# Seven half-size products in place of eight for the gate and up blocks of a two-layer diffusion backbone

## The chip, the cores and the metric

The kernel runs on one core of one Trainium2 chip. The time is the device time of one execution in microseconds (us), from runs of the whole program; the profile is one execution recorded by the hardware profiler. Engines are named as in the profile: PE (TensorE), PEld (its weight loads), DVE (VectorE), ACT (ScalarE), POOL (GpSimd) and SP (SyncE, which issues the DMAs).

## The reference

Two layers of a backbone over 640 tokens: 512 latent tokens and 128 context tokens, 1024 features each, which share all weights. Cut to what the change touches:

```python
D_MODEL = 1024; FFN_HIDDEN = 2816
def layer(x, cvec, p, rope, ctx_kv):
    sh1, sc1, g1, sh2, sc2, g2 = split(silu(cvec) @ p['w_ada'] + p['b_ada'], 6)
    h = rmsnorm(x, p['norm1_g']) * (1 + sc1) + sh1
    out, k, v = mixer(h, p, rope, ctx_kv)      # pooling, convolution, attention, gates, w_o
    x = x + g1 * out
    h2 = rmsnorm(x, p['norm2_g']) * (1 + sc2) + sh2
    ffn = (silu(h2 @ p['w_gate']) * (h2 @ p['w_up'])) @ p['w_down']
    return x + g2 * ffn, k, v
```

All of it is fp32. The last layer's output goes through one more norm.

## The kernel before

**Layout.** Activations lie transposed: features on the 128 partitions in 8 chunks (`KC`), the 640 tokens along the free axis, in two parts, `HALF` (384 and 256 tokens). A matmul takes 128x128 weights and one chunk of one part.

**Three products for one.** An fp32 value v is kept as a pair of fast-type (fp32r) numbers: hi = v rounded to that type, lo = v - hi. A product of two such values is taken as hi·hi + lo·hi + hi·lo, so each 128x128 weight tile and each activation chunk cost three matmuls per token part (`mm_op`, L425). The hi part is a cast on ACT (L365 for weights, L293 and L296 for activations), the lo part a subtraction, mostly on DVE (L369, L294, L297).

**Weights** stream in as blocks of 128 output columns (`Unit`, list `plan`): a DMA of 512 KB into one of 3 `RAW` buffers, then the split into one of 3 `WHL` slots, then 48 matmuls (8 chunks, 3 products, 2 parts). Blocks are used in the order of the plan.

**Feed-forward.** `w_gate` and `w_up` have 22 blocks each. `GROUPS` cuts them into 8, 8 and 6: in a group each gate block and its up block give two PSUM tiles, `hidden` turns them into one chunk of silu(gate)·up (tanh on ACT L1627, DVE L1628, DVE L1633, split L296 and L297), and then 8 blocks of `w_down` take the group's chunks to the residual stream, where DVE adds them with the gate factor (L1264, one instruction for the 512 latent and one for the 128 context tokens).

**Around it.** Ahead of the feed-forward stands a norm (`norm_half`, `norm_chunk`) that is taken part by part: while PE works on the residual blocks' second part, the first part's norm runs on DVE, ACT and POOL. `first_units` then takes three blocks (gate 0, up 0, gate 1) chunk by chunk as the norm delivers. The adaLN vectors of what is still to come (`ada_back`, L495: a 128x512 DVE instruction that multiplies and sums, and a small read of its accumulator behind it) are made during layer 0: 320 such instructions, put where DVE has nothing else.

**What sets the order.** Every engine's instruction order is fixed when the program is built: `_Order` runs a plain model of costs, and each engine takes the most urgent of the instructions that the model finds ready. Weight splits have a slack of 1500 ns (`WEIGHT`), ada work one of 1e7 (`BACK`), so it goes last. `dve_pool` lets the model choose between DVE and POOL by which would finish first. On the chip each engine follows its fixed list and waits on semaphores.

Of the kernel before, what the change touches and what calls it, by code (L numbers as in the profile page):

```python
# [1767 lines left out]
```

## Time and profile before

| | |
|---|---|
| time, median of 3 runs | 1947.42 us (1944.76 to 1949.25) |
| profiled execution: span, first to last instruction | 1945.7 us (1.7 us under the median) |
| PE busy | 1893.2 us, 97% |
| DVE, ACT, POOL busy | 1180.7, 651.3, 214.2 us |
| matmuls at L425 | 11520 of 12893 |
| span that the feed-forward stages take | about 433 us in layer 0, 442 us in layer 1 |

The time of the profiled execution apart from its span is not listed; the three runs lie within 0.23%. Read the table stage by stage: a busy share is a mean over stages in which different engines come last. A matmul's listed duration contains its pipeline, so the pace of PE is read from the starts of successive matmuls.

### The profile page before, as it was taken

Reading aid. Unit: us, or ns where it says so; the run is one execution under the profiler, and the core shown is the slowest. Engines: PE = TensorE matmul, PEld = TensorE weight load, DVE = VectorE, ACT = ScalarE, POOL = GpSimd, SP = SyncE. Lnnn points to the kernel's source line nnn. Section 1 sums busy time; section 2 is a strip of 40 time slices with the busy share of each in tenths; the row PEclk is TensorE's granted clock in tenths of the full one; section 3 lists DMA queues with packets and bytes.
Section 4 is the critical chain, followed back from the end, with each engine's and each line's share of the span. In section 5 each row is a group of like instructions: output and inputs, shape, how many; then the busy total and the mean of one; then the engine's idle time right before and its main releaser. Section 6 shows DMA issues by size and latency. Waiting matters only on the chain.

```text
span 1945.7 us, 31187 instructions
## 1 busy us (share of the span) xinstructions
PE 1893.2 (97%) x12893; PEld 1861.3 (96%) x12893; DVE 1180.7 (61%) x1998; ACT 651.3 (33%) x1039; POOL 214.2 (11%) x182
## 2 busy tenths in 40 slices
PE   6999999999999999999989999999999999999997
PEld 4888999999999999999989899999999999999997
DVE  7689868878777777763477985333347333333334
ACT  4466732222432122212244664222224221221223
POOL 3352000001200000000035400000012000000001
PEclk8999999999999999999998999999999999999998
DMA  7210135446234444432322101222322222222212
GB/s 274 96 46 29 44 122 159 159 157 212 92 128 148 148 147 153 150 130 71 116 80 70 41 28 44 86 72 77 115 97 76 77 73 71 74 76 76 77 60 71
DMA packets 74223, 195.79 MB, mean 101 GB/s; under 512 B 8545, under 2 KB 12641, under 8 KB 74081
## 3 DMA queue, kind: packets, MB, share of 16 engines
q1 hardware_dynamic: 74082, 193.81, 30.2%
q8 instruction: 101, 1.65, 0.4%
q14 instruction: 40, 0.33, 0.1%
HBM read 186.96 MB, written 5.51 MB: 99 GB/s over the span
## 4 chain that ended last, share of the span: by engine, by line
PE 85%; DVE 10%; issue 2%; ACT 2%; POOL 0%; DMA 0%; SPq 0%; DVEq 0%; ACTq 0%; POOLq 0%
PE ps L425 79%; PE ps L957 1%; PE ps L939 1%; DVE g L294 1%; PE ps L977 1%; DVE g L683 1%; DVE z L661 1%; DVE st L945 1%; DVE g L495 1%; PE ps L1412 1%; PE ps L750 1%; DVE t L641 0%; DVE z L791 0%; ACT p L947 0%; DVE p L276 0%
## 5 line engine op out<-in xcount | busy, mean ns | idle before, releaser
L425 PE MATMUL ps<-g,wh 128*128 128x256 f32 (+1 forms) x7552 | 1680.4, 310 | 3.4 <-DVE g L294 1.7
L425 PEld LDWEIGHTS ps<-g,wh 128*128 128x128 f32 x7552 | 1279.7, 190 | 4.9 <-issue 3.1
L425 PE MATMUL ps<-g,wl 128*128 128x384 f32 (+1 forms) x3776 | 1167.3, 309 | 1.9 <-DVE wl L369 1.9
L425 PEld LDWEIGHTS ps<-g,wl 128*128 128x128 f32 x3776 | 717.3, 190 | 2.5 <-DVE wl L369 2.4
L365 ACT CAST wh<-wr 128x1024 fp32r<-128x1024 f32 (+2 forms) x256 | 250.8, 981 | 546.2 <-PE ps L425 291.8
L369 DVE TENSOR_TENSOR wl<-wr,wh 128x1024 fp32r<-128x1024 f32 (+2 forms) x233 | 275.5, 1182 | 115.9 <-ACT wh L365 108.9
L1264 DVE SCALAR_TENSOR_TENSOR g<-ps,mod,g 128x128 f32<-128x128 f32 (+2 forms) x140 | 67.3, 518 | 166.1 <-PE ps L425 166.0
L495 DVE CUSTOM_DVE_ANT_0 junk<-p,k,vec 128x512 f32<-128x512 f32 x160 | 122.5, 766 | 33.8 <-DMA p<-in_w_ada 31.7
L495 DVE CUSTOM_DVE_ANT_0 junk<-p,k,part 128x512 f32<-128x512 f32 x160 | 120.2, 751 | 22.4 <-DMA p<-in_w_ada 18.1
L588 POOL TENSOR_TENSOR u<-u,t 128x256 f32<-128x256 f32 (+1 forms) x15 | 17.8, 1189 | 941.9 <-ACT t L583 941.9
L1633 DVE TENSOR_TENSOR t<-t,ps 128x640 f32<-128x640 f32 x44 | 36.1, 821 | 133.5 <-PE ps L425 133.5
L1628 DVE SCALAR_TENSOR_TENSOR t<-t,ps 128x640 f32<-128x640 f32 x44 | 35.9, 821 | 124.9 <-ACT t L1627 124.9
L1627 ACT ACTIVATE t<-ps 128x640 f32<-128x640 f32 x44 | 30.9, 707 | 220.2 <-PE ps L425 220.2
L1214 ACT ACTIVATE t<-ps 128x640 f32<-128x640 f32 x32 | 22.6, 707 | 192.0 <-PE ps L425 192.0
L1225 POOL TENSOR_TENSOR u<-u,t 128x640 f32<-128x640 f32 x12 | 22.8, 1903 | 516.3 <-ACT wh L365 268.8
L367 POOL TENSOR_TENSOR wl<-wr,wh 128x1024 fp32r<-128x1024 f32 x23 | 57.9, 2519 | 91.8 <-ACT wh L365 67.4
L947 ACT ACTIVATE p<-ps,st 128x640 f32<-128x640 f32 x64 | 50.9, 795 | 38.8 <-DVE st L945 34.4
L294 DVE TENSOR_TENSOR g<-ps,g 128x640 fp32r<-128x640 f32 (+1 forms) x68 | 54.8, 811 | 11.9 <-ACT g L293 11.5
L659 ACT ACTIVATE g<-t,mod,gain 128x128 fp32r<-128x128 f32 (+2 forms) x88 | 46.5, 574 | 32.7 <-DVE gain L1425 17.9
L425 PE MATMUL ps<-g,g 128*128 128x384 f32 (+1 forms) x192 | 45.5, 338 | 11.7 <-DVE g L683 6.6
L945 DVE TENSOR_REDUCE st<-ps 128x1 f32<-128x640 f32 x64 | 51.8, 815 | 6.5 <-PE ps L939 6.1
L641 POOL TENSOR_TENSOR t<-g,u 128x256 f32<-128x256 f32 (+2 forms) x37 | 50.0, 1355 | 44.4 <-DVE z L661 9.2
(146 smaller groups left out, 1292.0 us busy)
## 6 DMA issues: line engine op xcount, KB each, us to landing
p<-in_w_ada SPq DMA_DIRECT2D x160, 256.0 KB, 3.0
wr<-in_w_in SPq DMA_DIRECT2D x76, 512.0 KB, 3.4
wr<-in_w_gate SPq DMA_DIRECT2D x44, 512.0 KB, 3.3
wr<-in_w_up SPq DMA_DIRECT2D x44, 512.0 KB, 3.4
wr<-in_w_down SPq DMA_DIRECT2D x32, 512.0 KB, 3.3
g<-in_w_ada SPq DMA_DIRECT2D x16, 512.0 KB, 5.8
wr<-in_w_br SPq DMA_DIRECT2D x32, 256.0 KB, 2.7
wr<-in_w_o SPq DMA_DIRECT2D x16, 512.0 KB, 3.6
```

What stands on the lines that cost most here:

```text
L294: yield dve(n, lambda: nc.vector.tensor_sub(lo, src, hi))
L365: yield act(n, lambda: nc.scalar.copy(h, r), slack=WEIGHT)
L367: yield pool(n, lambda: nc.gpsimd.tensor_sub(w, r, h), slack=WEIGHT)
L369: yield dve(n, lambda: nc.vector.tensor_sub(w, r, h), slack=WEIGHT)
L425: nc.tensor.matmul(toks(ps, c0, n), lhsT=wt[:, c], rhs=xt[:, c0 : c0 + n], start=start and i == 0, stop=stop and i == 2,)
L495: return dve(n + 60, lambda: nc.vector.tensor_tensor_reduce(out=waste[:, :n], in0=w, in1=s, scale=0.5, scalar=start, op0=ALU.mult, op1=ALU ...
L641: f = lambda e: e.tensor_mul(t[:, :n], xk, r)
L659: nc.scalar.activation(out, sl, AF.Identity, bias=bias, scale=scale)
L945: yield dve(TOK, lambda: nc.vector.tensor_reduce(st[:, 0:1], toks(ps), axis=AX.X, op=ALU.max, negate=True))
L947: yield act(TOK + 140, lambda: nc.scalar.activation(pp, toks(ps), AF.Exp, bias=st[:, 0:1], accum_out=st[:, 1:2]))
L1264: yield dve(n, lambda: nc.vector.scalar_tensor_tensor(xs, toks(ps, s0, n), mods[l][:, v, seg * KC + m : seg * KC + m + 1], xs, op0=ALU.mul ...
L1633: yield dve(TOK, lambda: nc.vector.tensor_mul(t, t, toks(ps)))
```

## The change

`HALF` becomes 320 and 320 tokens; the norm's second and first parts of 320 are covered by three 128-token tiles each (`TILES`, two of them overlapping in the first part). `GROUPS` becomes 6, 6, 6, 4. From the third gate block on, a gate block and its up block are no longer two products. Stacked, they form a 2x2 block matrix: rows gate and up, columns the first and the last 512 input features (a11, a12, a21, a22); the activations form a 2x2 block matrix of feature halves by token parts (b11 to b22). Strassen's scheme in Winograd's form takes the block product with seven products of 4 chunks by 320 tokens instead of eight.

New work for that: per layer the sums t1 to t4 of the activations (`Quarters.combine`, split in `Quarters.parts`); per pair the sums s1 to s4 of the weights (`Pair.sums`), split as seven 512-wide quarters instead of two 1024-wide blocks (L351, L355); per pair the gathering of the results (`Seven.gather`): partial sums accumulate in PSUM, and in between are copied by ACT (L642) and added by DVE (L647). PE's product 6 waits for the copy of product 1, product 4 for the addition of product 7. `hidden_of` takes silu(gate)·up from the gathered tile.

The weight slots become 6 slots of 4 KB per partition (`WQ`; a pair needs 7, an ordinary block 2), raw buffers 4 instead of 3, large tiles 13 instead of 12. Comments are removed throughout, and those lines are left out here.

```diff
-HA = 384
+HA = 320
...
-GROUPS = ((0, 8), (8, 8), (16, 6))
+GROUPS = ((0, 6), (6, 6), (12, 6), (18, 4))
+PLAIN = 2
...
+TILES = {(0, TOK): (0, P, 2 * P, 3 * P, 4 * P), HALF[0]: (0, P, HA - P), HALF[1]: (HA, 3 * P, 4 * P)}
...
-    BIG, RAW, WHL, TT, ZZ, PP, UU, PS, MIX = (_Slots(order, n) for n in (12, 3, 3, 3, 2, 2, 4, 4, 1))
+    BIG, RAW, WQ, TT, ZZ, PP, UU, PS, MIX = (_Slots(order, n) for n in (13, 4, 6, 3, 2, 2, 4, 4, 1))
...
+    class Pair:
...
+        ORDER = ("a11", "s1", "s2", "a12", "s3", "s4", "a22")
...
+        def prepare(self, turn):
+            for e in self.loaded:
+                yield e
+            (_, r0), (_, r1) = self.raw
+            h = D // 2
+            self.part = {"a11": r0[:, :h], "a12": r0[:, h:], "a21": r1[:, :h], "a22": r1[:, h:]}
+            self.there = {q: event() for q in ("s1", "s2", "s3", "s4")}
+            self.parted = {q: event() for q in self.ORDER}
+            spawn(self.sums())
+            yield turn
+            for q in self.ORDER:
+                s = self.slot[q] = yield WQ.get()
+                t = mk("wq", s, (D,), F32R)
+                self.hi[q], self.lo[q] = t[:, :h], t[:, h:]
+                spawn(self.parts(q))
+            self.placed.fire()
+            for e in self.parted.values():
+                yield e
+            for s, _ in self.raw:
+                RAW.put(s)
+        def sums(self):
+            n = D // 2
+            p = self.part
+            freed = {"s1": ("s2",), "s2": ("s4",), "s3": (), "s4": ()}
+            for q, x, y, op in (
+                ("s1", "a21", "a22", ALU.add), ("s2", "s1", "a11", ALU.subtract),
+                ("s3", "a11", "a21", ALU.subtract), ("s4", "a12", "s2", ALU.subtract),
...
+                p[q] = u_t(s)[:, :n]
+                f = lambda e: e.tensor_tensor(p[q], p[x], p[y], op=op)
+                yield dve_pool(n, f, slack=WEIGHT)
+                self.there[q].fire()
+                after([self.parted[q]] + [self.there[r] for r in freed[q]], lambda s=s: UU.put(s))
+        def parts(self, q):
+            if q in self.there:
+                yield self.there[q]
+            yield from half_split(self.hi[q], self.lo[q], self.part[q], D // 2)
+            self.parted[q].fire()
+            self.ready[q].fire()
...
+        def free(self, q):
+            WQ.put(self.slot[q])
...
+            for j in range(g0, g0 + gn):
+                if j < PLAIN:
+                    plan += [Unit(a["w_gate"][l, j], big=j == 0), Unit(a["w_up"][l, j])]
+                else:
+                    plan.append(Pair(a["w_gate"][l, j], a["w_up"][l, j]))
             plan += [
-                Unit(a[n][l, g0 + j], big=g0 + j == 0 and n == "w_gate")
-                for j in range(gn) for n in ("w_gate", "w_up")
-            ]
-            plan += [
-                Unit(a["w_down8"][l, gi, m] if gn == 8 else a["w_down6"][l, m], gn * P) for m in range(KC)
+                Unit(a["w_down6"][l, gi, m] if gn == 6 else a["w_down4"][l, m], gn * P) for m in range(KC)
...
+    class Quarters:
...
+        def make(self):
+            self.z = []
+            for _ in range(2):
+                s = yield BIG.get()
+                self.zslots.append(s)
+                self.z.append(big_t(s, F32))
...
+        def combine(self):
...
+            steps = (("t1", "b12", "b11", "b11"), ("t2", "b22", "t1", None), ("t3", "b22", "b12", "b12"),
+                     ("t4", "b21", "t2", "b21"))
...
+                for c in (slice(0, 2), slice(2, 4)):
+                    yield dve_pool(2 * HA, lambda e: e.tensor_sub(b[q][:, c], b[x][:, c], b[y][:, c]))
+                split_up.append(spawn(self.parts(q, b[q])))
+            for d in split_up:
+                yield d
+            for z in self.zslots + [s]:
+                BIG.put(z)
+            self.freed.fire()
...
+        def parts(self, q, src):
+            s = yield BIG.get()
+            self.slots.append(s)
+            t = big_t(s).rearrange("p a b -> p (a b)").rearrange("p (i k n) -> p i k n", i=2, k=4)
+            self.tiles[q] = t
+            for c in (slice(0, 2), slice(2, 4)):
+                yield act(2 * HA, lambda: nc.scalar.copy(t[:, 0, c], src[:, c]))
+                yield dve(2 * HA, lambda: nc.vector.tensor_sub(t[:, 1, c], src[:, c], t[:, 0, c]))
+            self.ev[q].fire()
...
+    def product(out, w, q, x, t, start, stop):
...
+        done = event()
+        def f(k):
+            for i, (wt, lo) in enumerate(((w.hi, 0), (w.lo, 0), (w.hi, 1))):
+                nc.tensor.matmul(
+                    out, lhsT=wt[q][:, k * P : k * P + P], rhs=x.get(t, lo, k),
+                    start=start and k == 0 and i == 0, stop=stop and k == 3 and i == 2, skip_group_check=True,
+                )
+        for k in range(4):
+            yield pe(3 * HA, lambda: f(k), slack=MAIN, follow=True, done=done if k == 3 else None)
+        after([done], lambda: w.free(q))
+        return done
...
+        def run(self, x):
+            w = next(coming)
+            self.s0 = yield PS.get(0)
+            s1 = yield PS.get(0)
+            p0, p1 = ps_t(self.s0), ps_t(s1)
+            pa, pb, pc = p0[:, :HA], p0[:, 512 : 512 + HA], p1[:, :HA]
+            self.pa = pa
+            got = {n: event() for n in range(1, 8)}
...
+            def go(n, out, q, t, start, stop, wait=None):
+                if wait:
+                    yield kept[wait]
+                d = yield from product(out, w, q, x, t, start, stop)
+                after([d], got[n].fire)
+            yield from go(1, pa, "a11", "b11", True, True)
+            yield from go(5, pc, "s1", "t1", True, True)
+            yield from go(6, pa, "s2", "t2", False, True, 1)
+            yield from go(2, pb, "a12", "b21", True, True)
+            yield from go(7, pa, "s3", "t3", False, True, 6)
+            yield from go(3, pc, "s4", "b22", False, True, 5)
+            yield from go(4, pa, "a22", "t4", False, True, 7)
+            after([got[4]], self.c21.fire)
...
+        def gather(self, got, kept, pa, pb, pc, s1):
...
+            def keep(n, dst, src):
+                yield got[n]
+                yield act(HA, lambda: nc.scalar.copy(dst, src))
+                kept[n].fire()
+            def plus(n, dst, src):
+                yield got[n]
+                yield dve(HA, lambda: nc.vector.tensor_add(dst, dst, src))
+            def c11():
+                yield from keep(1, lo, pa)
+                yield from plus(2, lo, pb)
+            def c22():
+                yield from keep(5, y, pc)
+                yield from plus(7, y, pa)
+                kept[7].fire()
+                self.c22.fire()
+            def c12():
+                yield from keep(6, hi, pa)
+                yield from plus(3, hi, pc)
...
-            nt = n // P
+            at = TILES[c0, n]
+            nt = len(at)
...
+            hq = Quarters(h)
+            after([h.made], lambda q=hq: spawn(q.make()))
+            done = yield from with_norm(l, 1, 2, x, mg.mg, KC, stats, h, quarters=hq)
             after([done], mg.mg.free)
+            after([done], lambda q=hq: spawn(q.combine()))
...
                         quiet[0] = False
+                    if g0 + j >= PLAIN:
+                        seven = Seven()
+                        spawn(hidden_of(u, j, seven))
+                        used = yield from seven.run(hq)
...
+    def hidden_of(u, j, c):
+        yield c.first
+        i = yield TT.get()
+        t = t_t(i)
+        yield act(TOK, lambda: nc.scalar.activation(t, c.x, AF.Tanh, scale=0.5))
+        yield dve_pool(TOK, lambda e: e.scalar_tensor_tensor(t, t, 1.0, c.x, op0=ALU.add, op1=ALU.mult))
+        TT.put(c.xslot)
+        yield c.c22
+        yield dve_pool(HA, lambda e: e.tensor_mul(t[:, HA:], t[:, HA:], c.y))
+        ZZ.put(c.yslot)
+        yield c.c21
+        yield dve(HA, lambda: nc.vector.tensor_mul(t[:, :HA], t[:, :HA], c.pa))
```

In layer 0's feed-forward the list of DVE held, around one block (wl, wh: a weight block's lo and hi parts; p, k, part, mod: the ada work; ps: the products; g: the activation pairs):

```order
L1628 SCALAR_TENSOR_TENSOR t_5566<-t_5566,ps_5490 128x640
L369 TENSOR_TENSOR wl_5565<-wr_5468,wh_5564 128x1024
L495 ISA junk,part<-p_5533,k_2619,vec 128x512
L495 ISA part 128x1
L495 ISA junk,mod_75<-p_5549,k_2561,part 128x512
L495 ISA mod_75 128x1
L495 ISA junk,mod_75<-p_5549,k_2657,part 128x512
L495 ISA mod_75 128x1
L1633 TENSOR_TENSOR t_5566<-t_5566,ps_5560 128x640
L369 TENSOR_TENSOR wl_5631<-wr_5491,wh_5630 128x1024
L297 SCALAR_TENSOR_TENSOR g_5157<-t_5566,g_5147 128x640
```

This is the whole of a gate and up block's DVE work, with three ada instructions in between. In the change the same place of DVE's list reads (wq: a weight quarter's hi and lo parts; u: a sum of weights; z and t: the gathered results):

```order
L647 TENSOR_TENSOR z_6934<-z_6934,ps_6931 128x320
L446 TENSOR_TENSOR u_7049<-wr_6990 128x512
L355 TENSOR_TENSOR wq_7040<-wr_6844,wq_7040 128x512
L647 TENSOR_TENSOR t_6933<-t_6933,ps_6932 128x320
L446 TENSOR_TENSOR u_7058<-u_7049,wr_6988 128x512
L355 TENSOR_TENSOR wq_7059<-u_6943,wq_7059 128x512
L1916 SCALAR_TENSOR_TENSOR t_7069<-t_7069,t_6933 128x640
L446 TENSOR_TENSOR u_7088<-wr_6988,wr_6990 128x512
L355 TENSOR_TENSOR wq_7082<-u_6975,wq_7082 128x512
L1922 TENSOR_TENSOR t_7069<-t_7069,ps_6931 128x320
L446 TENSOR_TENSOR u_7111<-wr_6988,u_7058 128x512
L355 TENSOR_TENSOR wq_7100<-wr_6844,wq_7100 128x512
```

These twelve rows are about half of one pair's list; the ada rows stand in the other half. In the whole list of layer 0 a pair has seven L355, three L647 and one each of L1916, L1922 and L301, and the 20 pairs have 57 L446 together.

POOL's list of the same stage held nothing: its last row is the norm's, and the next one belongs to the residual at the layer's end (t, u: the norm's and the statistics' tiles):

```order
L641 TENSOR_TENSOR t_5314<-g_4624,u_4567 128x256
L641 TENSOR_TENSOR t_5334<-g_4624,u_4567 128x256
L641 TENSOR_TENSOR t_5348<-g_4624,u_4567 128x256
L641 TENSOR_TENSOR t_5368<-g_4624,u_4567 128x256
L588 TENSOR_TENSOR u_9096<-u_9096,t_9212 128x256
```

In the change it has, for the second group of pairs (u: sums of weights; L1919: silu times up for the second token part):

```order
L446 TENSOR_TENSOR u_6313<-u_6304,wr_6209 128x512
L1919 TENSOR_TENSOR t_6644<-t_6644,z_6506 128x320
L446 TENSOR_TENSOR u_6763<-wr_6708 128x512
L1919 TENSOR_TENSOR t_6793<-t_6793,z_6652 128x320
L446 TENSOR_TENSOR u_6831<-wr_6706,u_6784 128x512
L446 TENSOR_TENSOR u_6918<-u_6907,wr_6844 128x512
L1919 TENSOR_TENSOR t_6935<-t_6935,z_6792 128x320
L446 TENSOR_TENSOR u_6975<-wr_6844,u_6918 128x512
L1919 TENSOR_TENSOR t_7069<-t_7069,z_6934 128x320
L1919 TENSOR_TENSOR t_7207<-t_7207,z_7077 128x320
L1919 TENSOR_TENSOR t_7343<-t_7343,z_7215 128x320
```

In layer 0 it is 20 of the 20 L1919, 21 of the L446 behind the norm, and 3 of the activations' 8 sums (L544).

Behind the norm, DVE's list before went straight on to the first blocks' products (L1628, L1633) and the next weights:

```order
L1628 SCALAR_TENSOR_TENSOR t_5417<-t_5417,ps_5146 128x640
L1628 SCALAR_TENSOR_TENSOR t_5431<-t_5431,ps_5149 128x640
L1633 TENSOR_TENSOR t_5417<-t_5417,ps_5148 128x640
L369 TENSOR_TENSOR wl_5422<-wr_5104,wh_5421 128x1024
L297 SCALAR_TENSOR_TENSOR g_5157<-t_5417,g_5147 128x640
L369 TENSOR_TENSOR wl_5430<-wr_5162,wh_5429 128x1024
```

In the change the sums t1 to t4 (L544) and their lo parts (L559) come first, between the first quarters (L355):

```order
L544 TENSOR_TENSOR g_4578<-g_4578 128x2x320 x2
L1899 SCALAR_TENSOR_TENSOR t_5394<-t_5394,ps_5169 128x640
L544 TENSOR_TENSOR g_5388<-g_4579,g_4578 128x640
L1904 TENSOR_TENSOR t_5394<-t_5394,ps_5170 128x640
L559 TENSOR_TENSOR g_5412<-g_4578,g_5412 128x640
L355 TENSOR_TENSOR wq_5396<-wr_4985,wq_5396 128x512
L355 TENSOR_TENSOR wq_5397<-u_5163,wq_5397 128x512
L1899 SCALAR_TENSOR_TENSOR t_5436<-t_5436,ps_5171 128x640
L559 TENSOR_TENSOR g_5412<-g_4578,g_5412 128x640
L544 TENSOR_TENSOR g_4578<-g_4579,g_4578 128x2x320
L355 TENSOR_TENSOR wq_5435<-u_5189,wq_5435 128x512
L559 TENSOR_TENSOR g_5463<-g_5388,g_5463 128x640
```

The second lo part of t2, which product 6 of the first pair needs, stands five rows further down.

## Rows read from the trace of the kernel before

**Rows 1.** The page, busy time: us (share) xinstructions

```profile
PE 1893.2 (97%) x12893; PEld 1861.3 (96%) x12893; DVE 1180.7 (61%) x1998; ACT 651.3 (33%) x1039; POOL 214.2 (11%) x182
```

**Rows 2.** The page, chain that ended last: shares of the span

```profile
PE 85%; DVE 10%; issue 2%; ACT 2%; POOL 0%; DMA 0%; SPq 0%; DVEq 0%; ACTq 0%; POOLq 0%
```

**Rows 3.** Stretches: length, busy PE, PEld, DVE, ACT, POOL (xcount); clock, DMA, GB/s

```profile
539.00:972.00 433.00, 432.84 (x2955) 432.84 (x2956) 284.14 (x552) 97.98 (x121) 4.09 (x4) 1.00 0.41 133
1490.00:1932.00 442.00, 442.00 (x3023) 442.00 (x3022) 155.85 (x187) 103.43 (x134) 6.06 (x7) 1.00 0.22 71
```

**Rows 4.** Busy DVE of the ada line L495 in layer 0's feed-forward

```profile
539.00:972.00 433.00, 137.98 (x364) 1.00 0.41 133
```

**Rows 5.** Timeline of PE in layer 1's feed-forward: start, us, instruction

```profile
1599.83 0.28 PE L425 MATMUL ps<-g,wl 128*128 128x256 f32 x1
...
1600.19 0.28 PE L425 MATMUL ps<-g,wl 128*128 128x256 f32 x1
...
1600.61 0.34 PE L425 MATMUL ps<-g,wl 128*128 128x384 f32 x1
...
1601.13 0.34 PE L425 MATMUL ps<-g,wl 128*128 128x384 f32 x1
```

**Rows 6.** Timeline of DVE in layer 0's merge stage

```profile
308.31 0.69 DVE L369 TENSOR_TENSOR wl<-wr,wh 128x512 fp32r<-128x512 f32 x1
308.91 0.81 DVE L1219 SCALAR_TENSOR_TENSOR t<-t,ps 128x640 f32<-128x640 f32 x1
309.64 1.22 DVE L369 TENSOR_TENSOR wl<-wr,wh 128x1024 fp32r<-128x1024 f32 x1
310.78 2.07 DVE L495 CUSTOM_DVE_ANT_0 junk<-p,k,vec 128x512 f32<-128x512 f32 x1
...
312.89 0.75 DVE L495 CUSTOM_DVE_ANT_0 junk<-p,k,part 128x512 f32<-128x512 f32 x1
...
313.69 0.75 DVE L495 CUSTOM_DVE_ANT_0 junk<-p,k,part 128x512 f32<-128x512 f32 x1
```

**Rows 7.** Timeline of DVE in layer 0's feed-forward, one residual addition

```profile
640.81 1.01 DVE L1264 SCALAR_TENSOR_TENSOR g<-ps,mod,g 128x512 f32<-128x512 f32 x2 [0.68 <-PE ps L425]
641.74 0.74 DVE L495 CUSTOM_DVE_ANT_0 junk<-p,k,vec 128x512 f32<-128x512 f32 x1
```

**Rows 8.** Timeline of POOL: five instructions

```profile
106.09 1.29 POOL L789 TENSOR_TENSOR t<-t,g 128x512 f32<-128x512 f32 x1 [2.64 <-DVE st L950]
...
151.90 2.84 POOL L367 TENSOR_TENSOR wl<-wr,wh 128x1024 fp32r<-128x1024 f32 x1
...
309.80 2.50 POOL L1225 TENSOR_TENSOR u<-u,t 128x640 f32<-128x640 f32 x1 [54.00 <-DVE t L1219]
365.60 1.57 POOL L1225 TENSOR_TENSOR u<-u,t 128x640 f32<-128x640 f32 x1 [53.30 <-ACT wh L365]
...
490.83 0.74 POOL L588 TENSOR_TENSOR u<-u,t 128x256 f32<-128x256 f32 x1 [7.58 <-ACT t L583]
```

**Rows 9.** Timeline of DVE beside two of these

```profile
152.42 0.68 DVE L294 TENSOR_TENSOR g<-ps,g 128x512 fp32r<-128x512 f32 x1
...
365.63 2.62 DVE L369 TENSOR_TENSOR wl<-wr,wh 128x1024 fp32r<-128x1024 f32 x1 [0.17 <-ACT wh L365]
```

**Rows 10.** Stretches outside the feed-forward, columns as in rows 3

```profile
145.92:194.60 48.68, 45.90 (x323) 43.34 (x322) 43.91 (x73) 32.13 (x68) 12.21 (x18) 1.00 0.09 29
512.00:544.00 32.00, 30.60 (x201) 28.30 (x200) 27.93 (x58) 19.80 (x38) 12.92 (x11) 1.00 0.14 51
982.00:1016.00 34.00, 28.48 (x171) 25.87 (x172) 28.43 (x58) 17.64 (x36) 17.95 (x13) 0.95 0.31 97
1038.00:1040.00 2.00, 0.63 (x4) 0.31 (x2) 1.47 (x2) 1.98 (x3) 0.25 (x1) 1.00 0.55 134
1040.00:1048.00 8.00, 7.73 (x34) 7.73 (x34) 2.49 (x5) 4.38 (x9) 4.05 (x2) 0.57 0.23 75
1932.00:1946.00 14.00, 3.38 (x18) 2.72 (x16) 5.11 (x16) 1.89 (x5) 2.68 (x4) 0.61 0.52 187
```

More of the change, by code (lines that the diff above doesn't have):

```diff
@@ L311, in make @@
         def make(self):
-            for _ in range(2 * self.n):
+            for _ in range(-(-2 * self.n // 4)):
                 s = yield BIG.get()
@@ L407, in stream @@
                 yield u.gate
-            yield from u.load()
+            yield from u.load(turn)
+            turn = u.placed
     def weights():
@@ new lines, in product @@
+    def product(out, w, q, x, t, start, stop):
+        yield w.ready[q]
+        for e in x.there(t):
+            yield e
+        done = event()
[9 more added lines that the diff above has]
+        return done
@@ L683, in norm_chunk, with norm_half @@
         yield dve(n, lambda: nc.vector.tensor_sub(lo[:, c], z[:, c], hi[:, c]))
-        ZZ.put(z_slot)
         for half in halves:
             h.ev[half][k].fire()
-    def norm_half(l, which, x, stats, h, half):
+        if quarters:
+            for half in halves:
+                quarters.zev[half][k].fire()
+        else:
+            ZZ.put(z_slot)
+    def norm_half(l, which, x, stats, h, half, quarters=None):
         yield from stats.rstd(half)
@@ L696, in norm_half @@
             i = yield TT.get()
-            r = toks(ps, c0, n) if k == 0 else rt[:, c0 : c0 + n]
-            d = spawn(norm_chunk(l, which, x, k, r, h, c0, n, SEGS[half], (half,), read if k == 0 else None, i))
+            r = ps[:, c0 : c0 + n] if k == 0 else rt[:, c0 : c0 + n]
+            d = spawn(norm_chunk(l, which, x, k, r, h, c0, n, SEGS[half], (half,), read if k == 0 else None, i,
+                                 quarters=quarters))
             if k == 0:
-                yield act(n, lambda: nc.scalar.copy(rt[:, c0 : c0 + n], toks(ps, c0, n)))
+                yield act(n, lambda: nc.scalar.copy(rt[:, c0 : c0 + n], ps[:, c0 : c0 + n]))
                 after([read], lambda: PS.put(slot))
@@ L710, in final_half @@
         copied = event()
-        tasks = [spawn(final_chunk(x, k, toks(ps, c0, n), rt[:, c0 : c0 + n], copied, c0, n)) for k in range(KC)]
-        yield act(n, lambda: nc.scalar.copy(rt[:, c0 : c0 + n], toks(ps, c0, n)))
+        tasks = [spawn(final_chunk(x, k, ps[:, c0 : c0 + n], rt[:, c0 : c0 + n], copied, c0, n)) for k in range(KC)]
+        yield act(n, lambda: nc.scalar.copy(rt[:, c0 : c0 + n], ps[:, c0 : c0 + n]))
         copied.fire()
@@ L1573, in main @@
                 if last:
[L1574 removed]
+                    after([used], hq.free)
                     stats = Stats(quick=l + 1 == DEPTH)
@@ L1608, in normed @@
                 else:
-                    tasks.append(spawn(norm_half(l, which, x.chunk, stats, h, half)))
+                    tasks.append(spawn(norm_half(l, which, x.chunk, stats, h, half, quarters)))
                 yield tasks[-1]
@@ L1634, in hidden @@
         PS.put(s)
+        yield u.made
+        yield from split(u.hi(j), u.lo(j), t, TOK, scale=0.5)
+        TT.put(i)
+        u.fire(j)
+    def hidden_of(u, j, c):
[10 more added lines that the diff above has]
+        yield dve(HA, lambda: nc.vector.tensor_mul(t[:, :HA], t[:, :HA], c.pa))
+        PS.put(c.s0)
         yield u.made
```

176 lines of the change are left out of this document (129 added, 47 removed).

## The prediction

> **What bounds the kernel now.** I read the busy shares of the page first, then the chain of waits, then the two feed-forward stages as stretches, since the change lies there. PE is busy for 97% [rows 1] and carries 85% of the chain that ended last [rows 2]; the reader is to see that nothing else comes near. Inside the feed-forward it is sharper: in layer 0 PE is busy for 432.84 of 433.00 us, in layer 1 for 442.00 of 442.00 [rows 3]. So there a matmul taken away is time taken away, as long as PE stays the last. The same rows show who could take its place: DVE is busy for 284.1 us in layer 0's stretch, but for 155.9 us in layer 1's. The difference is the ada work, 138.0 us of DVE in layer 0 [rows 4]. Layer 0 has far less room for new DVE work.
>
> **What goes.** In full flow three matmuls of 256 columns start 0.36 us apart (1599.83 to 1600.19) and three of 384 columns 0.52 us apart (1600.61 to 1601.13) [rows 5]: 120 and 173.3 ns each. A straight line between them gives 146.7 ns at 320 columns, so two parts of 320 cost what 384 and 256 cost, and the new part size is free in full flow. A pair of blocks took 2 x 24 x (120 + 173.3) ns = 14.08 us; seven products of 4 chunks and 3 matmuls take 84 x 146.7 ns = 12.32 us. 1.76 us less for each of 40 pairs is **-70.4 us**, 35.2 us in each layer. All of it lies on the path.
>
> [...]
>
> **What DVE gets in layer 0.** Prices are distances between starts in a packed stretch [rows 6]: a 512-wide instruction 0.60 us (308.31 to 308.91), a 640-wide one 0.73, a 1024-wide one 1.14; from 512 and 640 I estimate 0.40 for 320. A residual addition takes 0.93 [rows 7]. An ada instruction with its read takes 0.80 (312.89 to 313.69). Per pair there go two 1024-wide lo parts and the two 640-wide readings of the products, 2 x 1.14 + 2 x 0.73 = 3.74 us. There come seven 512-wide lo parts (4.20), 57/20 sums (1.71), three additions of 320 (1.20), one of 640 (0.73) and one of 320 (0.40): 8.24 us. Net 4.5 us, 90 us for 20 pairs. The activation sums add 5 instructions and 8 lo parts of 640, 9.5 us. The fourth group adds 8 residual additions, 7.4 us, and 8 shorter weight splits, 0.5 us. DVE's need rises from 284.1 to **391.5 us**, against 432.8 - 35.2 = **397.6 us** of PE work. By itself that would just fit.
>
> It doesn't stand by itself. POOL had 4.1 us of work in this stretch [rows 3] and now gets 21 sums of 512, 20 products of 320 and 3 activation sums of 640. The trace shows what a POOL instruction does to DVE. At 365.60 POOL's 640-wide addition ran for 1.57 us, and the DVE subtraction begun beside it took 2.62 instead of 1.22 [rows 6, 8, 9]. At 309.80 DVE was first, POOL's same addition took 2.50, and the next DVE instruction 2.07 instead of 0.75. Either way the two take turns, and DVE loses POOL's own time less some 0.2 us. An instruction that takes one input from PSUM is not held: 0.68 us at 152.42, inside POOL's 2.84 from 151.90 [rows 8, 9]. POOL's own times are 1.29 us for 512 [rows 8], and by a line through 0.74 (256) and 1.57 (640) 0.88 for 320. DVE's losses: 21 x 1.09 + 20 x 0.68 + 3 x 1.37 = 40.6 us; a sixth of DVE's new list reads PSUM, so I count 34. DVE then needs 425 us for 397.6 us of PE work, and becomes the last.
>
> PE must wait for the difference, since the order is fixed: the ada instructions stand between the lo parts and additions that PE waits for, urgent or not. That is 28 us if DVE never idles. It will idle a little behind casts, POOL's products and ada loads. I take **+38 us**. Bounds: 0, if POOL's turns fall where DVE waits anyway (391.5 fits into 397.6); and 75, if DVE gets no further than its 43.91 of 48.68 us, 90%, in the attention stage [rows 10]: 425/0.902 = 471 us.
>
> **What else is added.**
> - Layer 1's pairs: DVE needs 155.9 + 97 (68 sums here) + 9.5 + 7.9 = 270 us of 407, so it isn't the last. Inside a pair, product 6 waits for ACT's copy of product 1 and product 4 for DVE's addition of product 7; between lies one product, 1.76 us. Behind the waiting addition on DVE stand lo parts of the next pair, which PE wants only some products later. An addition (0.40) behind one 512-wide lo part that POOL holds (0.60 + 1.09) just misses. **+5 us**, between 0 and 16 (0.8 for each of 20).
> - Layer 1's first pair: from the norm's last chunk PE has nine matmuls, one plain block and two products, 1.3 + 7.0 + 3.5 = 11.9 us, before product 6 wants t2. DVE has 13 instructions of 640 and 5 of 512 up to t2's last lo part, 12.5 us, and some 6 us of POOL's turns. **+6 us**, 0 to 12; in layer 0 this is inside the 38.
> - The norm between the layers: its cover was the residual's second part and the first blocks' first part, 3 x 18 x 0.120 + 3 x 24 x 0.1733 = 19.0 us; with 4 chunks and 320 tokens it is 5.3 + 10.6 = 15.8. PE already idles 5.5 of 34 us there at a clock of 0.95 [rows 10]. **+4 us**, 0 to 8. The feed-forward's own norms keep their cover (21.1 us) and idle 1.4 of 32 us now; with new sums in DVE's and POOL's lists I take **+1 us** each, -1 to 3.
> - The end: behind PE's last work lie up to 14 us with 5.11 us of DVE [rows 10]; a last part of 320 instead of 256 tokens adds a quarter: **+1 us**, 0 to 3.
> - Attention and merge: the same work in a newly fixed order and with one more raw buffer. 0, between -5 and 8; the nearest row is PE's idle 2.8 of 48.7 us there [rows 10]. DMA moves the same bytes.
>
> **Sum.** -70.4 + 38 + 5 + 6 + 4 + 2 + 1 = -14 us. On the span of 1945.7 us that is 1931.5. The median of the runs stands 1.7 us above the span, so **1933 us**, its own range 1916 to 1950.
>
> **Rivals.**
> - *VectorE keeps up.* DVE's ada instructions and POOL's turns fall into waits, as the 391.5 in 397.6 us allows; layer 0 loses 5 instead of 38 us: 1900 us. For it: the model put ada last, so in the model DVE had room for it. Against it: the turns on [rows 8, 9], which that model doesn't contain.
> - *VectorE falls behind for good, and the change costs time.* Place: layer 0's pairs. A DVE that is last also waits, for casts, for POOL's product before L1922, for ada loads; at the attention stage's 90% layer 0 loses 75 us: 1970 us. It decides from the point where layer 0's loss passes 52 us, that is DVE's share falls under 425/449.6 = 95%. For it: no stretch of before holds DVE above 90%. Against it: that stage is a chain of short steps, while here splits stand several products ahead.
> [...]
>
> **Numbers.** Forecast 0.50, VectorE keeps up 0.24, falls behind 0.21, clock 0.05. A measurement of this kernel can tell about 0.2%, 3.9 us, from no change. Faster by more: all of the second case and 0.80 of the first, 0.64. Within: 0.14 of the first and a little of the third, 0.10. Slower: the rest, 0.26. The range reaches to the second case's 1900 and to the lower half of the third: 1901 to 1963.
>
> **What would show it.** Right: matmuls at the new product line start 147 ns apart in full flow; layer 1's stretch falls by 20 to 30 us, layer 0's by none or a few; there DVE is busy for over 93%, PE waits for DVE's lo parts and additions with idle spread thinly, and DVE instructions beside POOL's take 0.7 to 1.4 us longer. Layer 0's stretch 30 us shorter, or DVE below 90% with PE full, would show the second case; a clock under 1 in layer 0's pairs the fourth. It is wrong at its root if layer 1's pairs take much more than 12.3 us.

## The result and the profile after

The changed kernel takes **1975.82 us** (median of 4 runs, 1975.49 to 1977.73) against 1946.24 us before: ratio 1.0155, 95% interval 1.0141 to 1.0169. That is 29.6 us slower, where 13 us faster was forecast, and 13 us beyond the upper end of the range. The profiled execution spans 1974.3 us.

Its busy shares and its chain, from the page, answer to [rows 1, 2]:

```profile
PE 1853.8 (94%) x12427; PEld 1798.0 (91%) x12427; DVE 1454.6 (74%) x2514; ACT 800.5 (41%) x1402; POOL 319.5 (16%) x255
...
PE 78%; DVE 15%; ACT 3%; issue 3%; POOL 0%; DMA 0%; SPq 0%; DVEq 0%; ACTq 0%; POOLq 0%
```

PE was busy for 97% and is so for 94%; DVE and ACT together now carry 18% of the chain instead of 12%. To see where, I cut each layer at its statistics matmuls (L867, the summing of squares for a norm, once for each token part). The rows below are stretches of the changed kernel: length, busy PE, PEld, DVE, ACT, POOL, clock, DMA, GB/s. The first two run from the second statistics of a feed-forward norm to the first statistics of the next norm, layer 0 and layer 1, and hold all 20 pairs. The next two lie between the two statistics of the feed-forward norms. The last is the end of layer 1's.

```profile
526.53:998.24 471.71, 438.70 (x2877) 424.31 (x2876) 428.39 (x829) 179.23 (x317) 78.00 (x54) 0.99 0.38 124
1491.16:1954.07 462.91, 433.53 (x2875) 420.95 (x2873) 306.17 (x478) 184.53 (x328) 54.22 (x38) 1.00 0.22 67
505.14:526.53 21.39, 17.62 (x110) 16.69 (x108) 18.22 (x27) 11.78 (x19) 11.39 (x9) 0.92 0.21 66
1468.76:1491.16 22.40, 18.75 (x109) 18.09 (x108) 18.13 (x27) 11.78 (x19) 11.30 (x9) 0.85 0.21 72
1483.60:1490.40 6.80, 6.15 (x23) 6.03 (x24) 5.42 (x9) 1.67 (x3) 1.74 (x2) 0.50 0.44 149
```

Compare the first two. Where PE idled for 0.16 us in layer 0 and not at all in layer 1 [rows 3], it now idles 33.0 us in layer 0 and 29.4 us in layer 1. In layer 0 DVE is busy for 91%, in layer 1 for 66%, and yet the two lose nearly the same. So a full DVE can't be the main cause. What stops PE stands in the page's row of the product line (busy, mean ns, idle before and what ended most of it):

```profile
L589 PE MATMUL ps<-g,wq 128*128 128x320 f32 x3360 | 517.6, 312 | 50.8 <-ACT t L642 25.3
```

and in the views of two lines, the copies' L642 and then the additions' L647, under "who waited for it (us, times)":

```profile
  PE ps L589: 25.3, 42
```

```profile
  PE ps L589: 24.1, 40
```

PE waits 42 times for a copy and 40 times for an addition: once for each in every one of the 40 pairs, and for two copies more, both in a layer's second pair. One pair of layer 1 shows which, on the timeline of all engines (start, duration, instruction, idle time before it and what ended that):

```profile
1640.95 0.43 ACT L642 COPY t<-ps 128x320 f32<-128x320 f32 x1 [0.63 <-PE ps L589]
...
1641.42 2.03 PE L589 MATMUL ps<-g,wq 128*128 128x320 f32 x12 [0.52 <-ACT t L642]
...
1643.49 0.49 DVE L647 TENSOR_TENSOR t<-t,ps 128x320 f32<-128x320 f32 x1 [0.87 <-PE ps L589]
...
1644.03 10.83 PE L589 MATMUL ps<-g,wq 128*128 128x320 f32 x72 [0.58 <-DVE t L647]
...
1654.90 0.43 ACT L642 COPY t<-ps 128x320 f32<-128x320 f32 x1 [0.95 <-PE ps L589]
...
1655.38 2.02 PE L589 MATMUL ps<-g,wq 128*128 128x320 f32 x12 [0.52 <-ACT t L642]
```

A product is 12 matmuls, so a pair shows as one product that stands alone and six in one run. The lone one starts when a copy into t is done, and only products 1 and 6 are copied into t; the run behind it starts when its own result is added to t, as only those of products 2 and 3 are. In the order 1, 5, 6, 2, 7, 3, 4 that leaves product 2 for the lone one. It waits for the copy of product 6, and product 7 waits for the addition of product 2. Neither wait is in the algorithm: product 2 writes `pb`, the copy reads `pa`. But `pa` and `pb` are the two halves of one PSUM tile, `p0`, as the diff's line `pa, pb, pc = p0[:, :HA], p0[:, 512 : 512 + HA], p1[:, :HA]` has it. From 1641.42 to 1655.38 a pair takes 13.96 us: the 12.32 of the forecast and 1.64 of waits. It took 14.08 before.

### The profile page after: what moved, and what is told of

Its sections match the earlier page's. It is cut to its first block, busy times and chain, and to the rows that moved or that the text cites. A ratio compares the mean times of both kernels' runs of the same rounds, so it can differ in the third digit from the quotient of the medians.

```text
span 1974.3 us, 31545 instructions
## 1 busy us (share of the span) xinstructions
PE 1853.8 (94%) x12427; PEld 1798.0 (91%) x12427; DVE 1454.6 (74%) x2514; ACT 800.5 (41%) x1402; POOL 319.5 (16%) x255
## 3 DMA queue, kind: packets, MB, share of 16 engines
q8 instruction: 97, 1.59, 0.3%
## 4 chain that ended last, share of the span: by engine, by line
PE 78%; DVE 15%; ACT 3%; issue 3%; POOL 0%; DMA 0%; SPq 0%; DVEq 0%; ACTq 0%; POOLq 0%
PE ps L679 49%; PE ps L589 23%; DVE wq L355 2%; PE ps L1202 1%; PE ps L1240 1%; DVE g L298 1%; PE ps L1220 1%; DVE t L647 1%; DVE g L941 1%; DVE junk L749 1%; ACT t L642 1%; DVE g L919 1%; DVE g L749 1%; DVE g L301 1%; PE ps L1675 1%
## 5 line engine op out<-in xcount | busy, mean ns | idle before, releaser
L679 PE MATMUL ps<-g,wq 128*128 128x320 f32 x7488 | 1150.4, 311 | 6.2 <-DVE g L301 3.6
L679 PEld LDWEIGHTS ps<-g,wq 128*128 128x128 f32 x7488 | 1109.8, 189 | 11.2 <-DVE g L301 4.9
L589 PE MATMUL ps<-g,wq 128*128 128x320 f32 x3360 | 517.6, 312 | 50.8 <-ACT t L642 25.3
L589 PEld LDWEIGHTS ps<-g,wq 128*128 128x128 f32 x3360 | 494.6, 188 | 72.8 <-ACT t L642 36.3
L351 ACT CAST wq<-wr 128x512 fp32r<-128x512 f32 (+2 forms) x312 | 244.7, 784 | 343.7 <-PE ps L679 240.6
L355 DVE TENSOR_TENSOR wq<-wr,wq 128x512 fp32r<-128x512 f32 (+2 forms) x289 | 266.6, 922 | 108.4 <-ACT wq L351 107.4
L1527 DVE SCALAR_TENSOR_TENSOR g<-ps,mod,g 128x128 f32<-128x128 f32 (+3 forms) x172 | 83.4, 522 | 107.8 <-PE ps L679 107.6
L351 ACT CAST wq<-u 128x512 fp32r<-128x512 f32 x160 | 98.5, 621 | 138.4 <-PE ps L589 79.6
L355 DVE TENSOR_TENSOR wq<-u,wq 128x512 fp32r<-128x512 f32 x160 | 128.2, 807 | 19.4 <-ACT wq L351 19.4
L1919 POOL TENSOR_TENSOR t<-t,z 128x320 f32<-128x320 f32 x37 | 46.2, 1250 | 512.0 <-DVE t L1916 512.0
L353 POOL TENSOR_TENSOR wq<-wr,wq 128x1024 fp32r<-128x1024 f32 x23 | 58.2, 2529 | 100.9 <-ACT wq L351 74.5
L647 DVE TENSOR_TENSOR t<-t,ps 128x320 f32<-128x320 f32 x80 | 38.8, 485 | 38.3 <-PE ps L589 37.9
L642 ACT COPY t<-ps 128x320 f32<-128x320 f32 x80 | 34.1, 426 | 80.0 <-PE ps L589 80.0
L917 ACT ACTIVATE g<-t,mod,gain 128x128 fp32r<-128x128 f32 (+5 forms) x98 | 52.1, 578 | 33.0 <-DVE gain L1688 14.7
L298 DVE TENSOR_TENSOR g<-ps,g 128x640 fp32r<-128x640 f32 x68 | 54.7, 809 | 8.4 <-ACT g L297 7.7
```

The costliest lines, as they stand in the source:

```text
L298: yield dve(n, lambda: nc.vector.tensor_sub(lo, src, hi))
L351: yield act(n, lambda: nc.scalar.copy(hi, src), slack=WEIGHT)
L353: yield pool(n, lambda: nc.gpsimd.tensor_sub(lo, src, hi), slack=WEIGHT)
L355: yield dve(n, lambda: nc.vector.tensor_sub(lo, src, hi), slack=WEIGHT)
L589: nc.tensor.matmul(out, lhsT=wt[q][:, k * P : k * P + P], rhs=x.get(t, lo, k), start=start and k == 0 and i == 0, stop=stop and k == 3 and ...
L642: yield act(HA, lambda: nc.scalar.copy(dst, src))
```

## The experiments

All ratios are against the kernel before, run on the same chip. Not all runs were on one chip; the kernel before took 1944.5 to 1946.2 us on them, so a difference between two of these kernels can be off by some 2 us.

**A tile of its own for product 2.** Every engine's order stays as it was.

```diff
-            pa, pb, pc = p0[:, :HA], p0[:, 512 : 512 + HA], p1[:, :HA]
+            pa, pb, pc = p0[:, :HA], p1[:, 512 : 512 + HA], p1[:, :HA]
```

> Edit: product 2 writes the second bank of the other PSUM tile (beside products 5 and 3) instead of the second bank of the tile that products 1, 6, 7 and 4 use. Nothing else moves: every engine keeps its order. Theory A (shared tile): of the two waits of each pair, the one of product 2 for ACT's copy of product 6, and the one of product 7 for DVE's addition of product 2, neither is in the algorithm; they come from two halves of one tile, and each stops PE for 0.76 us from start to start. Without them a pair falls from 13.9 to 12.4 us; 40 x 1.5 = 62 us less, 1914 us, or up to 20 us more than that if DVE is then the last in layer 0. Rival B (the chain of copies and additions inside a pair): the waits move to product 7 for the copy of product 6 and to product 4 for the addition of product 7, and the time stays within 10 us of 1976.

Measured: 1923.23 us, ratio 0.9892 (0.9876 to 0.9908), 52.6 us less than with the shared tile, and now faster than before. The timeline of a layer 1 pair:

```profile
1599.79 16.44 PE L589 MATMUL ps<-g,wq 128*128 128x320 f32 x111
1600.87 0.43 ACT L642 COPY t<-ps 128x320 f32<-128x320 f32 x1 [0.81 <-PE ps L589]
...
1602.63 0.49 DVE L647 TENSOR_TENSOR t<-t,ps 128x320 f32<-128x320 f32 x1
...
1613.19 0.43 ACT L642 COPY t<-ps 128x320 f32<-128x320 f32 x1 [0.19 <-PE ps L589]
```

PE runs 111 matmuls without a gap, across the copy of product 6 and the addition of product 2, which are unchanged in length. From one copy of product 6 to the next are 12.32 us, the forecast's figure to the last digit. The two stretches, as above:

```profile
528.03:976.95 448.92, 432.23 (x2877) 424.30 (x2876) 429.75 (x829) 178.06 (x317) 79.22 (x54) 0.99 0.39 130
1470.84:1902.43 431.59, 423.82 (x2874) 420.92 (x2873) 307.42 (x478) 184.40 (x328) 53.65 (x38) 1.00 0.22 72
```

Layer 1 is 31.3 us shorter (1.57 for each pair), layer 0 only 22.8. Theory A is shown, with its second half: in layer 0 something else now comes last. Rival B falls: the waits did not move to products 7 and 4, and in this pair the copies and additions that the algorithm needs are done before their next use.

**Parts and groups alone.** No block is taken as a pair.

```diff
-PLAIN = 2
+PLAIN = 22
...
-            hq = Quarters(h)
...
-            after([done], lambda q=hq: spawn(q.combine()))
...
-                after([hq.freed], lambda x=u: spawn(x.make()))
+                spawn(u.make())
```

> Edit: token parts of 320, groups 6, 6, 6, 4 and the enlarged pools stay, but every block is taken the plain way, with no sums and no products of halves. Theory A: the losses at the feed-forward norms (some 10 us at each) come from the pairs' weight sums and activation sums in DVE's and POOL's lists beside the norm; then parts and groups alone cost little, 1946 to 1954 us. Rival B: they come from the part size (two segments in the second part, less cover); then 1962 to 1972 us.

Measured: 1954.83 us, ratio 1.0050 (1.0033 to 1.0067), 10.3 us slower than before: 0.8 above the upper end of A, 7 below B. Its stretches (layer 0, layer 1, and the two norms):

```profile
528.49:986.37 457.88, 456.79 (x3113) 455.82 (x3112) 303.47 (x597) 110.23 (x152) 9.81 (x9) 1.00 0.39 128
1477.62:1935.03 457.41, 456.32 (x3109) 455.35 (x3108) 172.86 (x231) 115.14 (x163) 8.46 (x8) 1.00 0.20 67
...
509.58:528.49 18.91, 16.37 (x114) 16.07 (x113) 16.39 (x29) 10.59 (x17) 8.84 (x7) 1.00 0.18 58
1457.16:1477.62 20.46, 17.92 (x115) 17.65 (x114) 16.38 (x29) 10.59 (x17) 8.84 (x7) 0.92 0.22 77
```

These are the right base for the pairs. Less 35.2 us of products, the stretches of layer 0 and layer 1 would be 422.7 and 422.2. With product 2's own tile they stand 26.2 and 9.4 us above that, in the changed kernel 49.0 and 40.7. At the norms the pairs add 2.5 and 1.9 us (21.39 and 22.40 against 18.91 and 20.46). The kernel before has, at the same two norms:

```profile
509.44:527.59 18.15, 17.45 (x117) 16.50 (x116) 16.35 (x30) 11.82 (x18) 7.49 (x5) 1.00 0.24 88
1455.14:1473.33 18.19, 17.53 (x117) 16.57 (x116) 16.35 (x30) 11.82 (x18) 7.49 (x5) 1.00 0.25 87
```

So the changed kernel's norms are 3.2 and 4.2 us longer than before, where "some 10 us at each" was expected. The pairs make 2.5 and 1.9 of that; parts and groups alone make 0.8 and 2.3, so A's cause is a part of it only.

**DVE alone.** The tile of its own, and nothing of the pairs on POOL.

```diff
-                yield dve_pool(n, f, slack=WEIGHT)
+                yield dve(n, lambda: f(nc.vector), slack=WEIGHT)
...
-                    yield dve_pool(2 * HA, lambda e: e.tensor_sub(b[q][:, c], b[x][:, c], b[y][:, c]))
+                    yield dve(2 * HA, lambda: nc.vector.tensor_sub(b[q][:, c], b[x][:, c], b[y][:, c]))
...
-        yield dve_pool(HA, lambda e: e.tensor_mul(t[:, HA:], t[:, HA:], c.y))
+        yield dve(HA, lambda: nc.vector.tensor_mul(t[:, HA:], t[:, HA:], c.y))
```

> Edit: as own_tile, and the weight sums, activation sums, the tanh product and the y product run on DVE alone; POOL gets none of them. Theory A (turns of POOL and DVE cost DVE 34 us in layer 0 and hold the norm's chunks): 5 to 15 us less than own_tile, most of it at the two feed-forward norms and in layer 0's pairs. Rival B (DVE is full in layer 0 and needs POOL's help): 5 to 25 us more than own_tile, all in layer 0's feed-forward. Neither: within 4 us.

Measured: 1913.88 us, ratio 0.9843 (0.9828 to 0.9858), 9.3 us less than with POOL, as A said. Layer 0's stretch, the attention behind it, and layer 1's stretch of this kernel, and then the same attention with POOL's help:

```profile
525.61:962.80 437.19, 425.08 (x2878) 421.25 (x2876) 412.65 (x839) 180.33 (x317) 12.59 (x12) 1.00 0.39 131
...
982.82:1445.14 462.32, 444.88 (x3057) 439.42 (x3056) 275.03 (x413) 184.90 (x327) 74.24 (x66) 0.98 0.21 70
...
1465.17:1893.31 428.14, 423.00 (x2874) 420.93 (x2873) 300.33 (x508) 184.90 (x328) 8.16 (x8) 1.00 0.22 73
```

```profile
996.33:1449.95 453.62, 442.45 (x3053) 435.69 (x3052) 260.79 (x376) 185.45 (x325) 74.84 (x67) 0.99 0.20 68
```

Only a part came as expected. Layer 1's stretch falls by 3.5 us, and the two norms by 1.5 and 0.9 (from 21.59 and 20.89). Layer 0's falls by 11.7, but the next attention grows by 8.7: 14 us of DVE's work slipped out of layer 0 into it. So DVE is full in layer 0 with POOL or without (busy for 96% of its stretch and for 94%).

**Shorter ada instructions**, once with a tile of its own for product 2 and once with the shared tile.

```diff
-            out=waste[:, :n], in0=w, in1=s, scale=0.5, scalar=start, op0=ALU.mult, op1=ALU.add, accum_out=out,
+            out=waste[:, :64], in0=w[:, :64], in1=s[:, :64], scale=0.5, scalar=start, op0=ALU.mult, op1=ALU.add, accum_out=out,
```

> Edit: as own_tile, but each ada instruction reads 64 of its 512 columns (the rest of the modulation of the later stages is left out); its place in DVE's order is kept. DVE gets some 80 us less work in layer 0's feed-forward. Theory A (with the false waits gone DVE is the last in layer 0): 10 to 25 us less than own_tile, all in layer 0. Rival B (DVE keeps up in layer 0): within 4 us of own_tile.

> Edit: the changed kernel as it is (products 1, 6, 2, 7, 4 in one tile), but each ada instruction reads 64 of its 512 columns, as in own_tile_ada64; the rest of the modulation is left out. With a tile of its own for product 2 this edit took 20 us away. Theory A (the false waits slow PE, so DVE is hardly late): layer 0's waits in the changed kernel stand 8 us above layer 1's, so 6 to 11 us less than 1976, 1965 to 1970 us, and the waits at the copy and at the addition stay 0.76 us each. Rival B (DVE's lateness and the false waits add up): 20 us less, 1956 us.

Measured: 1903.19 us (0.9793, 0.9774 to 0.9812) and 1968.54 us (1.0114, 1.0097 to 1.0131): 20.0 and 7.3 us less than without the edit. Both times lie in theory A's range. The stretches of layer 0 and layer 1, with the own tile and with the shared one:

```profile
523.97:957.50 433.53, 425.98 (x2877) 422.85 (x2876) 353.35 (x829) 178.99 (x317) 77.29 (x54) 1.00 0.40 134
1449.52:1881.11 431.59, 423.82 (x2874) 420.91 (x2873) 307.00 (x478) 184.43 (x328) 54.27 (x38) 1.00 0.22 72
```

```profile
522.80:988.60 465.80, 436.83 (x2877) 424.24 (x2876) 348.61 (x829) 178.89 (x317) 76.33 (x54) 0.99 0.37 125
1484.00:1946.90 462.90, 433.55 (x2874) 420.95 (x2873) 306.24 (x478) 184.46 (x328) 54.24 (x38) 1.00 0.20 67
```

Layer 1, which has no ada work, doesn't move. Of the 20 us with the own tile, 15.4 lie in layer 0's stretch and 3.0 in the attention behind it (453.62 to 450.57). Layer 0's stretch falls from 448.92 to 433.53 us with the own tile, but by 5.9 with the shared one (471.71 to 465.80). With DVE's fill taken away, both layers lose the same to the shared tile: 32.3 and 31.3. So the false waits gave DVE time, and hid most of its lateness.

**Fewer pairs where DVE is full.** As the kernel with DVE alone, with the first pair of each layer at another block.

```diff
-PLAIN = 2
+PLAIN = (6, 2)
...
-                if j < PLAIN:
+                if j < PLAIN[l]:
...
-                    if g0 + j >= PLAIN:
+                    if g0 + j >= PLAIN[l]:
```

> Edit: as own_tile_dve, but in layer 0 the pairs begin at block 6 instead of 2 (16 pairs there, 20 in layer 1). Theory A (in layer 0 DVE is the last, and what it doesn't finish there it does in layer 1's attention): PE gets 4 x 1.76 = 7 us more, DVE some 22 us less; own_tile_dve lost about 10 us to DVE in layer 0's feed-forward and 12 in the stage after it, so 8 to 15 us less than its 1914: 1899 to 1906 us. Rival B (DVE's fill doesn't matter; the 12 us of the next attention come from the changed order): 7 us more than own_tile_dve, 1921 us.

> Edit: as before, with 12 pairs in layer 0. Theory A: PE 14 us more than own_tile_dve, and all of the 22 us that DVE cost are gone: 1906 us, that is a little behind the kernel with 16 pairs if that one has already room, ahead of it if not. Rival B: 1928 us.

> Edit: 16 pairs in layer 0 and 18 in layer 1. It tells what the first pair behind the norm costs in layer 1. Theory A (the activation sums are late for the first pair, 2.2 us at product 6 and something beside it): 1.5 to 3.5 us more than with (6, 2), since two pairs' 3.5 us are given up for a wait of 2. Rival B (the sums also hold the norm and the first blocks): 0 to 4 us less.

Measured: 1904.58 (0.9797, 0.9780 to 0.9814), 1909.20 (0.9815, 0.9799 to 0.9832) and 1904.39 us (0.9790, 0.9776 to 0.9805). The first is as theory A has it: four pairs fewer in layer 0 cost PE 7 us and save 16. The second stands 3 us above A's 1906: another four cost 7 and save 2. Of the kernel (6, 2), layer 0's stretch and the attention behind it, which is back at 450.6:

```profile
526.00:963.90 437.90, 432.04 (x2922) 429.51 (x2921) 403.31 (x822) 167.13 (x285) 11.85 (x11) 1.00 0.40 133
984.00:1434.60 450.60, 440.26 (x3053) 434.08 (x3052) 260.72 (x376) 185.68 (x325) 74.91 (x67) 1.00 0.20 68
```

The third stands 0.2 us from the first, which the intervals don't separate: A's 1.5 is not seen, and B holds at most at its edge. Two pairs given up in layer 1 cost PE 3.5 us and change nothing, so the first pairs behind a norm lose about what they save. With (6, 4) PE goes through layer 1's first two pairs in one run, without a wait:

```profile
1509.25 24.80 PE L589 MATMUL ps<-g,wq 128*128 128x320 f32 x168
```

(6, 2) and (6, 4) are the fastest of the versions that do all the work, about 2% faster than before.

## Why the prediction was wrong

**The step that failed** is "Inside a pair, product 6 waits for ACT's copy of product 1 and product 4 for DVE's addition of product 7; between lies one product", counted at +5 us, at most 16, in layer 1. These are the waits that the code writes down as events. The waits that come with the tiles were not looked for, though the diff shows products 6, 2 and 7 one behind the other in `p0`, with a reader of `p0` between each two. They cost 31.3 us in layer 1 and 22.8 in layer 0, where the sum had nothing for them. The waits that it did name cost little: with the own tile, layer 1 has one of them, 0.95 us in its second pair, and from then on PE runs through its pairs without a wait. Without them the kernel takes 1923.23 us, 10 us under the forecast; with them a pair takes 13.96 us against 14.08 before, and nothing is left to pay for the rest.

`pa` and `pb` share no column of `p0`: the one begins at column 0, the other at 512, and each is 320 wide. Product 2 waited for the copy of product 6 all the same, 0.52 us of idle at 1641.42, and the wait was gone when product 2 had another tile: 111 matmuls without a gap. So these waits go by the tile, whichever half is written.

**The products, −70.4 us**: right. 12.32 us a pair without the waits, and 111 matmuls in 16.44 us, of which the last is listed with 0.31, start (16.44 - 0.31) / 110 = 146.6 ns apart.

**DVE in layer 0, +38 us**: the mechanism was right, the size too high. With the own tile, DVE is busy for 96% of layer 0's stretch (429.75 of 448.92), and ada work taken from it gives 15.4 us back; in the changed kernel it is 5.9. The 38 also held the first pair: over the kernel without pairs, layer 0's stretch stands 26.2 us higher and the attention behind it 3.0 (453.62 against 450.6), 29 in all. A part of the excess is that DVE's need was set against PE's work over the 433 us of [rows 3] alone. The kernel before has between the same two statistics:

```profile
527.59:981.37 453.78, 453.07 (x3089) 451.73 (x3088) 297.02 (x579) 106.43 (x140) 10.58 (x11) 1.00 0.39 129
```

Over this stretch the same working gives 297 + 107 + 34 = 438 us against 453.8 - 35.2 = 418.6, a lack of 19 instead of 28. Whether the 10 us of idling put on top were there can't be told apart: DVE idled for 19.2 of the 448.92 us, and left ada work behind.

**POOL's turns, 34 us**: the turns are there (in a layer 1 pair of the changed kernel the lo part of a quarter begun at 1650.52, beside POOL's product of 1.19 us from 1650.14, took 1.37 us, the one at 1648.58 0.69), and POOL's help is worth nothing. Taking the pairs' work from POOL (79.22 to 12.59 us in layer 0) left DVE's busy time where it was: 429.75 + 260.79 = 690.5 us in layer 0's stretch and the attention with POOL, 412.65 + 275.03 = 687.7 without. I had expected DVE to lose 34 us to turns and to be spared some 23 by POOL (21 x 0.60 + 20 x 0.40 + 3 x 0.73), 11 net; it is 3 here, and 7 in layer 1 (307.42 against 300.33).

**Layer 1's pairs, +5, and its first pair, +6**: with the own tile PE waits in the first two pairs, 4.1 us in all, and then no more:

```profile
1504.27 3.78 PE L589 MATMUL ps<-g,wq 128*128 128x320 f32 x24 [1.02 <-DVE g L559]
1508.28 0.85 PE L589 MATMUL ps<-g,wq 128*128 128x320 f32 x4 [0.23 <-DVE g L559]
1510.02 7.30 PE L589 MATMUL ps<-g,wq 128*128 128x320 f32 x48 [0.88 <-DVE t L647]
1518.27 3.78 PE L589 MATMUL ps<-g,wq 128*128 128x320 f32 x24 [0.95 <-ACT t L642]
1523.09 30.22 PE L589 MATMUL ps<-g,wq 128*128 128x320 f32 x204 [1.04 <-ACT t L642]
```

Counted off by 12 for a product, these are: in the first pair products 6 and 7, which wait for the late sums (L559), 1.25 us, and product 3, which waits for the addition of product 2, as both now write `p1`, 0.88; in the second pair product 6 for the copy of product 1, 0.95, and product 7 for the copy of product 6, 1.04. So the late sums are there, at 1.25 us for the 6, and of the waits put at 5 only one, at 0.95. That layer 1's 9.4 us over the kernel without pairs come near 5 + 6 is partly luck, as a part of them lies outside these waits.

**The norms between the layers and at the end, +4 and +1, and the feed-forward's norms, +1 each**: together 7 were forecast, and parts and groups alone cost 10.3. Of these, 0.8 and 2.3 lie at the feed-forward norms; where the rest lies is not worked out here. The pairs add 2.5 and 1.9 us more there. One reason is on the timeline of the first of them: POOL puts a weight sum (L446) between two of the norm's multiplications, and DVE's split of a chunk beside it takes 1.59 us instead of 0.48.

```profile
514.84 0.48 DVE L941 TENSOR_TENSOR g<-g,g 128x320 fp32r<-128x320 f32 x1
...
516.03 1.38 POOL L446 TENSOR_TENSOR u<-wr 128x512 f32<-128x512 f32 x1
...
516.17 1.59 DVE L941 TENSOR_TENSOR g<-g,g 128x320 fp32r<-128x320 f32 x1
...
517.82 0.70 PE L679 MATMUL ps<-g,g 128*128 128x320 f32 x3 [1.55 <-DVE g L941]
...
519.50 1.14 DVE L941 TENSOR_TENSOR g<-g,g 128x320 fp32r<-128x320 f32 x1
...
520.70 0.86 PE L679 MATMUL ps<-g,g 128*128 128x320 f32 x3 [2.19 <-DVE g L941]
```

With DVE alone, where POOL has no weight sums, PE's first wait here is 0.44 us instead of 1.55; the second stays 2.19. So the second is not the weight sum's doing.

**The rivals.** "VectorE falls behind for good" gave 1970 us, near the time, and its sign was right, but by luck: the time came about in another way. Its place was layer 0's pairs and its price DVE's lateness; layer 1, with DVE at 66%, lost as much, and ada work made shorter took only 7.3 us off the changed kernel. A time that fits does not show a mechanism. A stretch of before does hold DVE above 90%, against what was said for this case: from 1070.08 to 1118.70 it was busy for 45.34 of 48.62 us, 93%. The case put down as "clock", at 0.05, had a clock under 1 in layer 0's pairs as its mark. The granted clock did fall at single gaps, but in one of these pairs only; most of the falls lie at the norms. From 1483.60 PE ran for 6.8 us at a granted clock of 0.50, in and behind a wait of 2.18 us that ended at 1484.25; the clock between the two statistics was 0.92 and 0.85, where such a norm had 1.00 before [rows 10], and 1.00 and 0.92 without pairs. In layer 1's pairs, where the one shown above has idles of 0.52 and 0.58 us, it stayed at 1.00. In layer 0's pairs it fell once, at the second pair, where PE waited 2.35 us for a copy: from 579 to 583 us it was 0.57, and the 12 matmuls behind the wait took 3.40 us. The same wait in layer 1 left it at 1.00, and there they took 2.02:

```profile
579.47 3.40 PE L589 MATMUL ps<-g,wq 128*128 128x320 f32 x12 [2.35 <-ACT t L642]
...
1543.40 2.02 PE L589 MATMUL ps<-g,wq 128*128 128x320 f32 x12 [2.36 <-ACT t L642]
```

So the clock cost 1.4 us in layer 0's pairs. "VectorE keeps up" fell: with the own tile it doesn't.

**The marks.** Of those named ahead, "wrong at its root if layer 1's pairs take much more than 12.3 us" is the one that came true, at 13.96.

## What to carry to other kernels

Write down, for each tile that several instructions share, who writes and who reads it in PE's order: in this program a reader between two products that wrote the same tile one behind the other was a wait of PE, 0.52 us at the copy and 0.58 at the addition, whatever halves they used. Alternate products between tiles, so that a copy or an addition, here 0.43 and 0.49 us, has one product's time to finish, here 1.76. When work is moved off PE, look first at the stage whose other engine has the least room, and move less there: 16 pairs in layer 0 were 9 us faster than 20, in the kernel with DVE alone.

## What the runs showed of the chip that was not expected

- An idle of PE cost more than its row says, in the layer 1 pair of the changed kernel shown above. The two waits of a pair are listed with 0.52 + 0.58 = 1.10 us, but the pair is 1.64 us longer. The two runs of matmuls between the gaps are listed with 2.03 and 10.83 us, 0.27 more each than 12 and 72 starts at 146.7 ns. Of this 0.16 is the last matmul, listed with 0.31; the rest stands at the first one behind a gap, whose successor starts 0.25 us after it instead of 0.147. From starts to starts is the safe way to measure.
- POOL's share of the elementwise work did not unload DVE: with 66.6 us of POOL's time in layer 0's stretch (79.22 against 12.59), DVE was busy 3 us longer over this stretch and the attention behind it than when it did all of it alone, and with 45.5 us in layer 1 (53.65 against 8.16) 7 us longer.
